# A quarter turn of an 8192 x 8192 matrix: two instead of five TensorE outputs in the last macro tile but one, and GpSimd and TensorE loops of seven turns

## The chip, the cores and the metric

The kernel runs on one core of a Trainium2 chip. The metric is the device time of one execution in microseconds (us). Three runs of the kernel before took 1258.8 to 1259.03 us, with a median of 1258.96 us. A profile is one more execution of the same program, recorded instruction by instruction and DMA packet by DMA packet; its own time is given beside its span.

## The reference

What is computed is a rotation by a quarter turn of a float32 matrix. There is no arithmetic in it, only movement: 256 MiB are read and 256 MiB are written.

```python
x = np.random.randn(8192, 8192).astype(np.float32)   # k = 1
def reference(x, k):
    return np.rot90(x, k)
```

Row r and column c of the input go to row 8191 - c and column r of the output. So the kernel has to transpose and to reverse the order of the columns.

## The kernel before

**Tiling.** The matrix is cut into 16 macro tiles of 1024 rows by 4096 columns (`macros`, numbered kk = 0 to 15). A macro tile is loaded in 8 loads of 128 rows by 4096 columns, 2 MiB each (t = 0 to 7), and stored in 8 outputs (j = 0 to 7), each 512 rows of the result by 1024 columns, also 2 MiB. Loads are numbered m = 8 kk + t and outputs n = 8 kk + j, both from 0 to 127. Output n needs a part of all 8 loads of its macro tile. In the steady state the outputs of one macro tile are made while the next one is loaded, so output n goes with load m = n + 8.

**Memory.** There are two landing buffers for loads and three buffers for outputs, 2 MiB each (`bufs`), and `ring`, which holds one macro tile, less one chunk, as 63 chunks of 128 rows by 512 columns. VectorE takes a landed load out of its landing buffer into the ring, with the columns reversed (`landed` has a step of -1). The chunk that does not fit into the ring (t = 7, j = 7) is reversed in place in its landing buffer, and TensorE transposes it from there into `corner`, a piece of PSUM.

**Two ways to make an output.** `by_pe(kk)` says which of the 8 outputs of a macro tile TensorE makes.

- By TensorE: VectorE copies the chunks into the ring; TensorE transposes 32 blocks of 128 x 128 against an identity matrix into the two halves of PSUM (`ps0`, `ps1`); ScalarE copies each filled part to the output buffer (an eviction); then ScalarE issues the store.
- Moved: VectorE transposes the chunks within squares of 32 x 32 on their way into the ring (`in_quadrants`); then 16 copies, each of a band of 32 partitions, bring the squares to their places in the output buffer: 3 by VectorE, 8 by GpSimd, 5 by ScalarE (`moves`, `pairs`). Outputs with j = 7 have 7 tiles in such a copy instead of 8, and the corner is evicted by ScalarE.

In macro tiles 0 and 15 TensorE makes all outputs, in 1 to 13 outputs 0 and 4, and in 14 outputs 0, 2, 4, 6 and 7.

**Order of the work.** Each engine's order is written out by hand.

- SyncE (`by_sync`) issues the loads. Load m waits until VectorE has taken everything out of the same landing buffer (`taken`).
- VectorE (`by_vector`) goes by loads. For load m it first makes its 3 copies of output n = m - 8, if that is a moved one; then waits for the landing; then waits until GpSimd's copies of output n are done (`s_pool`), or, for an output by TensorE, until its transposes are done (`s_half`); then takes the load out, in pieces, each of which counts up `s_rev`. Only then may a chunk of the ring be overwritten, since the ring holds one macro tile.
- GpSimd (`by_gpsimd`) goes by moved outputs: it waits until the output buffer is free (`room_for`), copies 7 times, waits for ScalarE's copies of the same output (`s_act`), and copies once more.
- TensorE (`by_tensor`) goes by its outputs in the order of `in_turn`. For the first two outputs of macro tile 15, `FIRST` = 120 and 121, parts are interleaved: two parts of output 120 (16 and 12 blocks, from loads 120 to 126), a part of 16 blocks of output 121, the last 4 blocks of output 120 (from load 127), and the rest of output 121.
- ScalarE (`by_scalar`) goes by outputs: it makes its share of copies or its evictions, and issues the store. For a moved output it waits, ahead of the store, for the first piece that VectorE takes out of load n + 8: `e.wait_ge(s_rev, rev[n + T, pieces[n + T][0][0]])`. That one wait stands for VectorE's and GpSimd's copies of output n.

All of ScalarE's work for output 120 stands behind the store of output 119.

**Loops.** The instructions of GpSimd, VectorE and TensorE are first recorded (`Program`) and then played. Macro tiles `first` to `first + 2 * times - 1` become a loop of `times` turns of two macro tiles; the rest is written out straight. In a loop every turn must have the same list of operations, and only the numbers that are waited for go up. GpSimd's loop goes over macro tiles 1 to 12, that of VectorE and that of TensorE over 2 to 13. ScalarE has no loop. `once` leaves out a wait for a number that has been waited for before.

A line of the profile such as L104 is the place in `Op.run` from which all recorded operations are issued, so the profile's groups are told apart by engine, operation and tile.

Of the kernel before, what the change touches and what calls it, by code (L numbers as in the profile page):

```python
# [13 lines left out]
J = W // (G * P)  # L14
# [10 lines left out]
BY_PE = [0, 4]  # L25
# [148 lines left out]
def kernel(tc: tile.TileContext, x: bass.AP, k: bass.AP, out: bass.AP):  # L174
    nc = tc.nc
# [6 lines left out]
    KK = len(macros)  # L182
# [13 lines left out]
    def by_pe(kk):  # L196
        if kk in (0, KK - 1):
            return list(range(J))
        return BY_PE if kk < KK - 2 else [*range(0, J, 2), J - 1]

    def in_quadrants(kk, j):
        return j not in by_pe(kk)

    moved = [in_quadrants(kk, js[0]) for kk, _, js, _ in outs]
# [36 lines left out]
    def moved_until(n):  # L241
        return sum(moved[: n + 1])

    def turned_until(n):
        return sum(len(parts[i]) for i in range(n + 1) if i in parts)
# [16 lines left out]
    s_rev = nc.alloc_semaphore("s_rev")  # L262
# [8 lines left out]
    def load_buf(m):  # L271
        if m < T:
            return m % (LAND + OUTS)
        return LAND + 2 if m == T else (m - T - 1) % LAND
# [10 lines left out]
    def once(e):  # L285
        seen = {}

        def wait(sem, n):
            if seen.get(sem, 0) < n:
                seen[sem] = n  # L290
                e.wait_ge(sem, n)

        return wait

    def room_for(wait, n):
        b = out_buf(n)
        stores = [i for i in range(n) if out_buf(i) == b]
        loads = [i for i in range(n_load) if load_buf(i) == b]
        if stores:
            wait(s_store[b], 16 * len(stores))  # L300
        elif loads:
            taken(wait, loads[-1])

    def tight(n):
        return J <= n < n_out - J and n % J == TIGHT
# [24 lines left out]
    for m in range(n_load):  # L330
        kk, t = divmod(m, T)
# [16 lines left out]
    def at(v, first, dims):  # L348
        return bass.AP(
            tensor=v.tensor, offset=v[:, first : first + 1].offset, ap=[v.ap[0], *dims]  # L350
        )

    def landed(b, js):
        return at(bufs[b][:], (js[0] + 1) * CH - 1, [*strides(js, CH), [-1, CH]])

    def chunk(kk, t, js):
        if (kk, t, js[0]) == (KK - 1, T - 1, J - 1):
            return at(ring[:], 0, [[CH, 1], [1, CH]])
        places = [slot(kk, t, j) for j in js]
        assert max(places) < SLOTS  # L360
        return at(ring[:], places[0] * CH, [*strides(places, CH), [1, CH]])

    def moves(n, share):
        kk, ts, (j,), _ = outs[n]
        rows = len(ts) * P
        places = [slot(kk, t, j) for t in ts if (t, j) != (T - 1, J - 1)]
        ((step, tiles),) = strides(places, CH)
        for a, q in share:
            yield (
                at(  # L370
                    bufs[out_buf(n)][q * Q : q * Q + Q, :],
                    a * Q,
                    [[rows, G], [P, tiles], [1, Q]],
                ),
                at(
                    ring[a * Q : a * Q + Q, :],
                    places[0] * CH + q * Q,
                    [[P, G], [step, tiles], [1, Q]],
                ),
            )  # L380
# [26 lines left out]
    def landings(m):  # L407
        return 16 * sum(1 + (i in BOTH) for i in range(m + 1) if load_buf(i) == load_buf(m))

    def turned_in(n):  # L410
        kk, _, (j,), _ = outs[n]
        return rev[kk * T + T - 1 - (j == J - 1), j]
# [37 lines left out]
    def by_vector(e):  # L450
        wait = once(e)
        for m in range(n_load):
            kk, t = divmod(m, T)
            e.part(kk)
            b = load_buf(m)
            n = m - T
            if n >= 0 and moved[n]:
                room_for(wait, n)
                wait(s_rev, turned_in(n))
                for to, of in moves(n, pairs[:BY_DVE]):  # L460
                    i = e.tensor_copy(out=to, in_=of)
                i.then_inc(s_dve, 1)
            e.wait_ge(s_land[b], landings(m))
            if n >= 0:
                if moved[n]:
                    e.wait_ge(s_pool, moved_until(n))
                    e.wait_ge(s_dve, moved_until(n))
                else:
                    e.wait_ge(s_half, turned_until(n))
            for js in pieces[m]:  # L470
                if (m, js[0]) == (n_load - 1, J - 1):
                    e.wait_ge(s_half, turned_until(KK * J - J))
                if kk < KK - 1 and (t, js[0]) == (T - 1, J - 1):
                    wait(s_rev, rev[m, 0])
                    e.tensor_copy(
                        out=at(bufs[b][:], 0, [[CH, 1], [1, CH]]), in_=landed(b, js)
                    ).then_inc(s_rev, 1)
                    continue
                turn = e.transpose if in_quadrants(kk, js[0]) else e.tensor_copy
                turn(out=chunk(kk, t, js), in_=landed(b, js)).then_inc(s_rev, 1)  # L480

    def in_turn():
        for n in parts:
            if n == FIRST[0]:
                early, late = parts[n], parts[FIRST[1]]
                yield n, early[:2]
                yield FIRST[1], late[:1]
                yield n, early[2:]
                yield FIRST[1], late[1:]
            elif n != FIRST[1]:  # L490
                yield n, parts[n]

    def by_tensor(e):
        e.part(-1)
        wait = once(e)
        e.wait_ge(s_id, 2)
        used = {}
        for n, some in in_turn():
            kk, ts, js, blocks = outs[n]
            e.part(kk)  # L500
            rows = len(ts) * P
            order = [(part, f) for part in some for f in part[2]]
            if js[0] == 0 and kk < KK - 1:
                late = parts[n][-1]
                order.sort(key=lambda o: (o[0] == late, o[1] % rows, o[1]))
            last = dict(order)
            for part, f in order:
                _, h, cols = part
                j, off = blocks[f // rows]
                t = ts[f % rows // P]  # L510
                if kk < KK - 1 and js[0] == 0 and f == parts[n][-1][2][0]:
                    m = kk * T + T - 1
                    wait(s_rev, rev[m, J - 1])
                    wait(s_freed, kk)
                    for g in range(G):
                        i = e.transpose(
                            corner[:, g * P : g * P + P],
                            bufs[load_buf(m)][:, g * P : g * P + P],
                            ident,
                        )  # L520
                    i.then_inc(s_corner, 1)
                if n == KK * J - J and h:
                    wait(s_freed, KK - 1)
                if used.get(h, part) != part:
                    wait(s_ev, evicted[used[h][0]] + 1)
                wait(s_rev, rev[kk * T + t, j])
                if part == parts[n][0] and f == last[part] and n != FIRST[1] and not tight(n):
                    room_for(wait, n)
                to = cols.index(f) * P
                i = e.transpose(  # L530
                    ps[h][:, to : to + P],
                    chunk(kk, t, [j])[:, 0, off : off + P],
                    ident,
                )
                if f == last[part]:
                    i.then_inc(s_half, 1)
                    used[h] = part
# [48 lines left out]

    by_sync(nc.sync)
    for e, by, first, times in (
        (nc.gpsimd, by_gpsimd, 1, 6),
        (nc.vector, by_vector, 2, 6),  # L590
        (nc.tensor, by_tensor, 2, 6),
        (nc.scalar, by_scalar, None, 0),
    ):
        program = Program()
        by(program)
        program.play(nc, e, first, times)
# [39 lines left out]
```

## Time and profile before

| what | value |
|---|---|
| median of three runs | 1258.96 us |
| the profiled execution | 1259.08 us |
| its span (first to last record) | 1257.8 us |
| VectorE (DVE) busy | 793.8 us, 63% |
| GpSimd (POOL) busy | 744.0 us, 59% |
| ScalarE (ACT) busy | 599.6 us, 48% |
| TensorE (PE) busy | 302.9 us, 24% |
| read and written in HBM | 268.44 MB each, 427 GB/s over the span |
| loads and stores, issue to landing | 15.0 and 15.8 us (medians) |
| chain that ended last | DMA 71%, DVE 14%, ACT 4%, POOL 4% |

How to read it: the page divides the span into 40 slices of 31.4 us; digits are busy tenths of a slice, and the row of the clock is the TensorE clock that was granted, in tenths of full speed. The timeline lists instructions of one engine in order of time: start in us, duration, engine and line, operation and tiles, the count of merged instructions, and in brackets the idle time before and what ended it. ACTq and SPq are the sequencers of ScalarE and SyncE, which issue DMAs. A load or store is 128 rows of 16,384 bytes or as much, 8 packets for each of the core's 16 DMA engines; the trace holds each packet's start and duration and the moment at which each engine reports its share as landed.

### The profile page before, as it was taken

To read this page: it belongs to the slowest core of one execution; us is meant where nothing else is said; L and a number is where in the kernel's file an instruction comes from. 1 tells how busy PE (TensorE), PEld (TensorE's weight loads), DVE (VectorE), ACT (ScalarE), POOL (GpSimd) and SP (SyncE) were. 2 spreads that over 40 slices of the span, in tenths; PEclk is the share of its full clock that TensorE was granted. 3 is DMA by queue.
4 is the path that set the end of the run, shared out by engine and by line. 5 is a ranking of instruction groups with operands and counts; after the bars stand their busy time and mean duration, and the time that the engine had idled before them with its cause. 6 is when DMAs were issued, how large, how long until landed. Compare 5 with 4: busy or idle time off the path is not lost.

```text
span 1257.8 us, 6012 instructions
## 1 busy us (share of the span) xinstructions
PE 302.9 (24%) x1556; PEld 264.8 (21%) x1556; DVE 793.8 (63%) x535; ACT 599.6 (48%) x556; POOL 744.0 (59%) x654
## 2 busy tenths in 40 slices
PE   1555013130131301313022130221302213024273
PEld 0454012130121301212012120121202212024273
DVE  2544866668666676666867667676677766764410
ACT  0334364463644636446364453645535455355364
POOL 0001966668666686666956668576685766965500
PEclk9987556555555555555556555565555556555597
DMA  9999999999999999999999999999999999999999
GB/s 400 420 430 429 429 429 429 429 431 430 430 430 429 430 428 430 428 430 430 430 430 429 431 428 431 428 430 428 430 430 429 430 429 431 427 423 428 427 428 381
DMA packets 36946, 537.09 MB, mean 427 GB/s; under 512 B 4160, under 2 KB 4160, under 8 KB 4160
## 3 DMA queue, kind: packets, MB, share of 16 engines
q10 hardware_dynamic: 19184, 278.93, 52.2%
q1 hardware_dynamic: 17744, 257.96, 48.0%
q8 instruction: 7, 0.11, 0.0%
q14 instruction: 11, 0.09, 0.0%
HBM read 268.44 MB, written 268.44 MB: 427 GB/s over the span
## 4 chain that ended last, share of the span: by engine, by line
DMA 71%; DVE 14%; ACT 4%; POOL 4%; issue 3%; PE 2%; ACTq 0%; DVEq 0%; SPq 0%; POOLq 0%
DMA buf<-in_x_dram 57%; DMA out_dram<-buf 14%; DVE ring L104 14%; ACT buf L104 4%; POOL buf L104 4%; PE ps L104 2%; ACTq L104 0%; DVE buf L104 0%; DVEq L101 0%; SPq L391 0%; DVEq L145 0%; POOLq L101 0%; SPq L311 0%; POOLq L151 0%; SPq L419 0%
## 5 line engine op out<-in xcount | busy, mean ns | idle before, releaser
L104 POOL COPY buf<-ring 32x1024 f32<-32x1024 f32 (+1 forms) x648 | 743.3, 1147 | 440.4 <-DMA out_dram<-buf 244.2
L104 ACT COPY buf<-ring 32x1024 f32<-32x1024 f32 (+1 forms) x405 | 414.8, 1024 | 324.2 <-DVE ring L104 292.5
L104 PE MATMUL ps<-head,ring 128*128 128x128 f32 x1496 | 290.7, 372 | 889.4 <-ACT buf L104 535.8
L104 PEld LDWEIGHTS ps<-head,ring 128*128 128x128 f32 x1496 | 255.3, 197 | 921.5 <-ACT buf L104 548.7
L104 DVE COPY ring<-buf 128x1024 f32<-128x1024 f32 (+5 forms) x152 | 157.7, 1044 | 415.6 <-DMA buf<-in_x_dram 320.1
L104 DVE STREAM_TRANSPOSE ring<-buf 128x3072 f32<-128x3072 f32 (+2 forms) x125 | 358.0, 2872 | 0.0
L104 ACT COPY buf<-ps 128x2048 f32<-128x2048 f32 (+4 forms) x149 | 183.3, 1278 | 313.6 <-DMA out_dram<-buf 149.3
L104 DVE COPY buf<-ring 32x1024 f32<-32x1024 f32 (+1 forms) x243 | 289.5, 1192 | 2.2
L104 PE MATMUL ps<-head,buf 128*128 128x128 f32 x60 | 15.2, 401 | 46.3 <-DVE buf L104 46.3
L104 PEld LDWEIGHTS ps<-head,buf 128*128 128x128 f32 x60 | 9.7, 199 | 52.0 <-issue 44.6
L104 DVE COPY buf<-buf 128x512 f32<-128x512 f32 x15 | 5.8, 387 | 0.0
L104 ACT ACT_TABLE_LOAD x1 | 1.3, 1283 | 3.4 <-PEq L419 3.4
L104 POOL MEMSET head<- 128x128 f32 x1 | 0.2, 204 | 2.9 <-POOLq L419 2.9
L104 POOL TENSOR_SCALAR_AFFINE_SELECT head<-head 128x128 f32<-128x128 f32 x1 | 0.3, 293 | 0.2 <-POOL head L104 0.2
L617 POOL MEMSET const-float32-0.0<- 128x1 f32 x1 | 0.1, 98 | 0.2 <-issue 0.2
L104 ACT COPY head<-head 128x1 f32<-128x1 f32 x1 | 0.2, 191 | 0.0
L617 POOL MEMSET const-bfloat16-1.0<- 128x1 bf16 x1 | 0.1, 100 | 0.0
L617 POOL MEMSET const-uint8-127<- 128x1 uint8 x1 | 0.1, 100 | 0.0
L617 POOL MEMSET const-float32-1.0<- 128x1 f32 x1 | 0.1, 98 | 0.0
## 6 DMA issues: line engine op xcount, KB each, us to landing
out_dram<-buf ACTq DMA_DIRECT2D x128, 2048.0 KB, 15.8
buf<-in_x_dram SPq DMA_DIRECT2D x121, 2048.0 KB, 15.0
buf<-in_x_dram ACTq DMA_DIRECT2D x3, 2048.0 KB, 16.9
buf<-in_x_dram SPq DMA_DIRECT2D x4, 1024.0 KB, 16.1
buf<-in_x_dram ACTq DMA_DIRECT2D x4, 1024.0 KB, 16.4
```

The lines of the kernel that those rows point to most:

```text
L104: i = getattr(e, self.name)(*self.args, **kwargs)
L617: nc = _bacc.Bacc("TRN2", target_bir_lowering=False, num_devices=1)
```

## The change

In macro tile 14 TensorE makes outputs 0 and 4, as in 1 to 13; outputs 2, 6 and 7 become moved ones. GpSimd's loop goes over macro tiles 1 to 14 in 7 turns, TensorE's over 1 to 14 instead of 2 to 13; VectorE's is as it was. So that every turn has the same list of operations, TensorE forgets at output 8 which numbers it has waited for. VectorE waits, ahead of its copies of a moved output, for the largest count that any moved output of the macro tile needs, instead of the one that this output needs.

```diff
@@ by_pe @@
         if kk in (0, KK - 1):
             return list(range(J))
-        return BY_PE if kk < KK - 2 else [*range(0, J, 2), J - 1]
+        return BY_PE
@@ by_vector @@
             if n >= 0 and moved[n]:
                 room_for(wait, n)
-                wait(s_rev, turned_in(n))
+                wait(s_rev, max(turned_in(i) for i in range(n - n % J, n - n % J + J) if moved[i]))
                 for to, of in moves(n, pairs[:BY_DVE]):
@@ by_tensor @@
             kk, ts, js, blocks = outs[n]
             e.part(kk)
+            if n == J:
+                wait = once(e)
             rows = len(ts) * P
@@ at the end of tile_rot90_kernel @@
-        (nc.gpsimd, by_gpsimd, 1, 6),
+        (nc.gpsimd, by_gpsimd, 1, 7),
         (nc.vector, by_vector, 2, 6),
-        (nc.tensor, by_tensor, 2, 6),
+        (nc.tensor, by_tensor, 1, 7),
         (nc.scalar, by_scalar, None, 0),
```

## The prediction

> **What bounds the kernel now.** I read the slices of the page first, then the chain of waits, then the end in windows of 10 us, then the timelines of ScalarE, GpSimd, VectorE and TensorE over the last macro tiles, and last the records of transfers and packets. The page's slices:
>
> ```profile
> PEclk9987556555555555555556555565555556555597
> DMA  9999999999999999999999999999999999999999
> GB/s 400 420 430 429 429 429 429 429 431 430 430 430 429 430 428 430 428 430 430 430 430 429 431 428 431 428 430 428 430 430 429 430 429 431 427 423 428 427 428 381
> ```
>
> The DMA engines are busy from end to end, and the chain of waits is 71% DMA. No compute engine exceeds 63%. The packet records say it more sharply. A packet of 16,384 bytes starts 3 ns before the one ahead of it on its engine ends, so the records fall into sixteen chains, one for each DMA engine. Each holds about 2048 packets of 0.611 (load) or 0.616 us (store), with hardly a hole. The engines end between 1253.7 and 1257.3 us, and the landing record follows 0.4 us later, 1257.7. So nothing that happens on compute engines costs time unless it leaves DMA engines without a queued transfer, and little can be gained: the sixteen chains hold about 1255 us each.
>
> The end in windows (us, then busy time and count of PE, PEld, DVE, ACT, POOL, then the granted TensorE clock, the DMA share and GB/s):
>
> ```profile
> 1190.00:1200.00 10.00, 5.04 (x25) 4.61 (x25) 2.47 (x2) 4.89 (x5) 0.00 (x0) 0.52 1.01 428
> 1200.00:1210.00 10.00, 6.65 (x57) 5.88 (x56) 2.41 (x3) 5.98 (x5) 0.00 (x0) 1.00 1.00 428
> 1210.00:1220.00 10.00, 8.23 (x72) 7.45 (x71) 1.59 (x2) 7.85 (x5) 0.00 (x0) 1.00 1.01 426
> 1220.00:1230.00 10.00, 8.96 (x79) 8.24 (x77) 0.00 (x0) 8.59 (x5) 0.00 (x0) 1.00 1.01 425
> ```
>
> GpSimd is done, TensorE runs at the full clock, and DMA has no hole. The place where a hole can open is the hand-over from output 119 (last of macro tile 14) to output 120 (first of 15), after the last load landed at 1209.13. ScalarE's timeline there:
>
> ```profile
> 1196.09 0.55 ACTq L104 DMA_DIRECT2D out_dram<-buf  x1
> ...
> 1203.07 0.55 ACTq L104 DMA_DIRECT2D out_dram<-buf  x1
> 1203.94 3.21 ACT L104 COPY buf<-ps 128x2048 f32<-128x2048 f32 x2 [0.90 <-PE ps L104]
> 1210.39 0.58 ACT L104 COPY buf<-ps 128x512 f32<-128x512 f32 x1 [3.24 <-PE ps L104]
> 1211.01 0.55 ACTq L104 DMA_DIRECT2D out_dram<-buf  x1
> 1211.65 3.63 ACT L104 COPY buf<-ps 128x2048 f32<-128x2048 f32 x2 [0.67 <-ACT buf L104]
> ```
>
> The three issues are stores 118, 119, 120. Two evictions of output 120 are done before the last load lands; only a third of 0.58 us follows it. The DMA engines reach store 120's packets at 1214.4 to 1216.9, so the issue at 1211.01 has 3.4 us to spare (less the start-up below). Later issues come every 4.25 us, and an engine takes 4.91 us for its part of a store, so the reserve then grows.
>
> **The change part by part.** In macro tile 14 outputs 2, 6 and 7 leave TensorE and become moved ones. Removed: 96 transposes and their ScalarE evictions (3.70 us for each of outputs 2 and 6). Added: 24 GpSimd copies, 9 VectorE copies, 15 ScalarE copies, and wider VectorE transposes for loads 112 to 119. A load with two outputs by TensorE costs VectorE a copy and a transpose of 3072 (2872 ns mean); loop turns do this at 429 to 430 GB/s, so loads 112 to 119 cost nothing; load issues keep 5 us or more of queued load.
>
> What counts is that a moved output's store waits, in ScalarE's order, for VectorE's first piece of load n+8, and VectorE starts that piece only after GpSimd's last copy of output n. GpSimd in the last macro tile now:
>
> ```profile
> 1138.11 11.63 POOL L104 COPY buf<-ring 32x1024 f32<-32x1024 f32 x8 [8.21 <-DMA out_dram<-buf]
> 1157.66 21.13 POOL L104 COPY buf<-ring 32x1024 f32<-32x1024 f32 x15 [7.92 <-DMA out_dram<-buf]
> 1186.81 1.03 POOL L104 COPY buf<-ring 32x1024 f32<-32x1024 f32 x1 [8.02 <-ACT buf L104]
> ```
>
> Outputs 113, 115, 117 come singly, with holes of 8 us. One takes 11.63 us here: seven copies of 1.03 or 1.40 and one of 3.00 beside VectorE's 128x4096 copy. Loads land every 9.78. With the change they come as 113-114-115 and 117-118-119.
>
> First row, from 1138.11: ends 1149.7, 1161.4, 1173.1. Loads 122 and 123 landed at 1160.07 and 1169.85, so VectorE is 1.3 and 3.2 us late; stores 114 and 115 go out at 1163.8 and 1175.5 (before: 1156.95, 1172.56). Store 114 moves until 1177.15 and load 124 until 1179.59 on the last engine, so at most half a microsecond of hole on fast engines: priced at nothing, since they end 3 us ahead of the slowest. If that cover were gone it would cost those 0.5 us.
>
> Second row. Output 117 ends at 1187.84 as now (its eighth copy waits for ScalarE). Output 118 follows: +11.7 = 1199.6; load 126 landed 1199.25. Load 126's VectorE copy then meets GpSimd's first copy of output 119 and ends about 1202.9 rather than 1201.57; store 118 issues at 1203.0. Output 119 has copies of seven tiles: 0.93 or 1.23, and about 2.9 beside the 128x4096 copy, 10.8 in all: 1210.5 (ScalarE's own part ends at 1208.9). So GpSimd, not the landing at 1209.13, releases the last load. VectorE's first piece 0.44: ScalarE issues store 119 at 1211.05.
>
> Then all of output 120's evictions lie behind that wait, which they did not before. Issue and start of a copy 0.60: 1211.65. First eviction (2048) 1.82: 1213.5. That frees the half of PSUM that TensorE needs for 16 transposes of output 121, which stand ahead of the last 4 of output 120. Their price has two ends in this trace:
>
> ```profile
> 1058.58 5.45 PE L104 MATMUL ps<-head,ring 128*128 128x128 f32 x28 [0.68 <-ACT buf L104]
> ...
> 1205.86 1.97 PE L104 MATMUL ps<-head,ring 128*128 128x128 f32 x16 [0.65 <-ACT buf L104]
> 1209.73 0.63 PE L104 MATMUL ps<-head,ring 128*128 128x128 f32 x4 [1.90 <-DVE ring L104]
> ```
>
> At the half clock (first line, a hand-over inside the loop) one takes 0.195 us, so 20 take 3.9; at full clock 2.6. Now TensorE works on outputs 118 and 119 ahead of 120; after the change it has nothing between output 116 and 120 and pauses again from about 1210 to 1213.5. In the loop the clock record goes to 1.0 for 3.4 us, then back to 0.5 after such a pause. I take the half clock: 1217.45 (full: 1216.15). Last eviction 0.58: **store 120 issues at 1218.1** (full clock 1216.8).
>
> From issue to first packet: the launch's first load, on empty engines, is issued at 0.91 and its sixteen first packets start at 1.96 to 2.52, that is 1.05 to 1.6; I take 1.3. So store 120's packets start at 1219.4, where the engines ran out of store 119 at 1217.3 to 1217.5 (1211.05 + 1.3 + 4.91, or on the slowest what was queued). From there an engine needs 39.26 us for its eight parts (so it does now), and 41.22 if a page of TensorE's code is fetched through it meanwhile: now two engines in the tail have that, a packet of 0.95 us and a hole of 1.0 after it. TensorE's pages come every 125 transposes or so (the records have them after 100, 229, 372, and behind the loop 471, 588, 729 of the program's transposes), and outputs 120 to 127 hold 256, so one still falls in the tail. Now the slowest engine is another (40.41, from 1216.90, delayed by ScalarE's pages); the one that takes TensorE's page becomes the slowest. 1219.4 + 41.2 + 0.4 for the landing = 1261.0, against 1257.7: **+3.3 us**.
>
> The other edits. Loop turns of TensorE and GpSimd over 1 to 14: some register instructions, on engines that are idle (TensorE 24% busy); no more than tenths of a microsecond each way, hidden behind DMA. VectorE's two waits on its own counter become one, for pieces finished a load earlier; a wait in the chain is 0.02 to 0.05 us. TensorE's forgotten waits at output 8 are for events long past. About two of the 7 TensorE pages go and a GpSimd page; the slowest engine took none of them, so 0, with 2 us as the end if it had.
>
> **The rivals.**
> - *Quick hand-over, no measurable difference.* If GpSimd is done by the landing and TensorE has the full clock: store 119 at 1209.75, store 120 at 1215.5, packets at 1216.8, end 1258.4: +0.7. It decides at an issue of store 120 at 1217.3: below, the loss is under 2.5 us. For it: full clock at 1200 to 1230 now, and each GpSimd row is my sum, not a row of the trace. Against: the clock in the loop's hand-over, and the copies of 3.00. Between the two lies +2.0 (GpSimd late, full clock).
> - *A second gap.* Output 121 needs 16 more cold transposes and its second eviction: issue about 1223.2, packets 1224.5, while store 120 is through at 1224.3. With first packets at 1.06 instead of 0.61 us, as at launch: +4.5.
> - *Code loading.* TensorE's loop body (136 transposes) begins 68 transposes earlier, and might straddle pages so that each turn fetches. The row: over 230 to 1100 us the instruction queue of TensorE moved nothing, in six turns whose body is longer than a page. If two pages were fetched in each of seven turns, 14 times 1.96 us over sixteen engines is one or two for each: another +2 to +4.
>  The Trainium skill ("Runtime: NRT & Kernel Launch", Instruction fetch mechanics) says that a taken branch whose target is outside the two-page window forces a fetch, and prefers unrolling. By that rule this change costs in each turn; the trace's six silent turns speak against it.
> - *Faster.* If a page less falls on the slowest engine: -1 to -2 us at most, and only with the quick hand-over.
>
> That the change does not do what it says is excluded by the order of instructions: the built kernel's loops and copies are as described.
>
> **How the numbers follow.** The profiled execution took 1259.08 us, with a span of 1257.8; the median is 0.12 lower. 1259.08 + 3.3 - 0.12 = 1262.3; I say 1262.2. 0.2% is 2.5 us, about what a measurement here can tell from no change. Chances: forecast 0.45, second gap 0.07, code loading 0.04: slower 0.56. Quick or half-quick hand-over 0.42: same. Faster 0.02. The range runs from the quick hand-over, 1259.6, to just short of the second gap's full price, 1263.6.
>
> **What would show it.** In the changed profile: GpSimd busy to about 1210.5; VectorE waiting there for GpSimd, not for the load; stores 119 and 120 issued near 1211 and 1218; TensorE's clock near half between 1210 and 1217; the DMA share of 1210 to 1220 near 0.6 instead of 1.01; and pure stores from there at the old pace. If the DMA share stays at 1 there, the hand-over was covered and the forecast is wrong. If the instruction queue of TensorE shows tens of packets, it was code loading. A loss before 1200 us would be a step that I priced at nothing.

## The result, and the profile after

The changed kernel takes 1264.31 us (median of 6 runs, 1262.97 to 1265.18) against 1258.88 (6 runs, 1258.55 to 1259.03). The ratio is 1.0042, 95% interval 1.0031 to 1.0053: slower by 5.4 us, where 3.3 were forecast, and outside the stated range. The profiled execution, 1265.18 us with a span of 1263.9, is the longest of the six.

The page's slices of the changed kernel show where the time went. Until about 1137 us (slice 36) they are within 2 GB/s of those of before; then the rate falls.

```profile
DMA  9999999999999999999999999999999999999989
GB/s 398 422 431 431 428 429 428 431 430 428 429 429 431 430 428 429 429 431 431 428 429 430 431 430 429 429 430 430 431 428 429 430 431 430 426 421 415 403 369 393
```

In windows of 10 us (columns as in the prediction), the first two lines from the kernel before, the others from the changed one:

```profile
1160.00:1170.00 10.00, 2.71 (x16) 2.47 (x14) 7.31 (x5) 2.86 (x3) 9.73 (x7) 0.67 1.00 424
1170.00:1180.00 10.00, 0.90 (x4) 0.71 (x4) 2.53 (x1) 2.82 (x2) 8.54 (x7) 0.50 1.01 424
```

```profile
1150.00:1160.00 10.00, 0.00 (x0) 0.00 (x0) 7.16 (x4) 5.21 (x5) 9.71 (x8) 0.50 1.02 421
1160.00:1170.00 10.00, 0.00 (x0) 0.00 (x0) 7.45 (x4) 5.21 (x5) 9.73 (x7) 0.50 0.97 385
1170.00:1180.00 10.00, 0.00 (x0) 0.00 (x0) 3.16 (x1) 1.45 (x1) 9.65 (x9) 0.50 0.97 377
...
1210.00:1220.00 10.00, 7.23 (x40) 6.99 (x38) 2.11 (x3) 5.00 (x4) 3.24 (x4) 0.69 0.77 328
1220.00:1230.00 10.00, 7.94 (x69) 7.14 (x68) 0.41 (x1) 7.87 (x5) 0.00 (x0) 1.00 0.80 337
```

There are two troughs. The second, 1210 to 1230, is the hand-over of the forecast: the DMA share (second number from the end) falls to 0.77 and 0.80. The first, 1160 to 1180, was priced at nothing. The share there hides most of it: it is 0.97, but the rate is 377 to 385 instead of 424 GB/s. The packet records say why. Of 492 load packets begun between 1150 and 1187 us, 86 took 0.70 to 2.0 us instead of 0.61 (before the change 7 of 499); all 86 began within 6 us of the issue of load 123, 124 or 125. That is 2.2 us per engine, in which it counts as busy and moves less. Idle time is another 0.9 us.

GpSimd, ScalarE and VectorE in this stage:

```profile
1137.55 44.54 POOL L104 COPY buf<-ring 32x1024 f32<-32x1024 f32 x31 [8.06 <-DMA out_dram<-buf]
1188.28 1.04 POOL L104 COPY buf<-ring 32x1024 f32<-32x1024 f32 x1 [6.18 <-ACT buf L104]
1191.20 22.16 POOL L104 COPY buf<-ring 32x1024 f32<-32x1024 f32 x16 [1.89 <-DMA out_dram<-buf]
```

```profile
1175.86 0.55 ACTq L104 DMA_DIRECT2D out_dram<-buf  x1
...
1205.88 0.55 ACTq L104 DMA_DIRECT2D out_dram<-buf  x1
...
1213.91 0.55 ACTq L104 DMA_DIRECT2D out_dram<-buf  x1
1214.50 3.21 ACT L104 COPY buf<-ps 128x2048 f32<-128x2048 f32 x2 [2.69 <-DVE ring L104]
1220.42 0.59 ACT L104 COPY buf<-ps 128x512 f32<-128x512 f32 x1 [2.71 <-PE ps L104]
1221.03 0.55 ACTq L104 DMA_DIRECT2D out_dram<-buf  x1
```

```profile
1172.67 3.16 DVE L104 COPY ring<-buf 128x4096 f32<-128x4096 f32 x1 [4.22 <-POOL buf L104]
...
1213.45 2.10 DVE L104 COPY ring<-buf 128x512 f32<-128x512 f32 x2 [3.79 <-POOL buf L104]
```

The four issues are stores 115, 118, 119 and 120. VectorE waits for GpSimd, not for the load, both in the first row (load 123) and at the last load. GpSimd's 24 copies of outputs 113 to 115 and the first 7 of output 117 run without a hole; its second row, outputs 118 and 119, starts at 1191.20, released by a store (115, which landed at 1191.05; before the change it landed at 1186.96), and ends at 1213.36. Store 120 is issued 7.1 us after store 119, at 1221.03, and by then the engines are empty. They were empty once before: of the 4.4 us for which an engine stands idle here, half lies ahead of store 119's first packets and half ahead of store 120's.

### The profile page after: what moved, and what is told of

It reads as the page before. It is cut to its first block, busy times and chain, and to the rows that moved or that the text cites. A ratio compares the mean times of both kernels' runs of the same rounds, so it can differ in the third digit from the quotient of the medians.

```text
span 1263.9 us, 5913 instructions
## 1 busy us (share of the span) xinstructions
PE 288.2 (23%) x1464; PEld 252.8 (20%) x1464; DVE 791.7 (63%) x538; ACT 604.0 (48%) x562; POOL 765.7 (61%) x678
## 4 chain that ended last, share of the span: by engine, by line
DMA 71%; DVE 13%; POOL 5%; issue 4%; ACT 4%; PE 1%; ACTq 0%; DVEq 0%; POOLq 0%; SPq 0%
DMA buf<-in_x_dram 56%; DMA out_dram<-buf 15%; DVE ring L104 13%; POOL buf L104 5%; ACT buf L104 4%; PE ps L104 1%; ACTq L104 0%; DVEq L101 0%; DVE buf L104 0%; POOLq L101 0%; SPq L391 0%; POOLq L151 0%; POOLq L145 0%; SPq L419 0%; ACTq L101 0%
## 5 line engine op out<-in xcount | busy, mean ns | idle before, releaser
L104 POOL COPY buf<-ring 32x1024 f32<-32x1024 f32 (+1 forms) x672 | 765.0, 1138 | 444.2 <-DMA out_dram<-buf 235.6
L104 ACT COPY buf<-ring 32x1024 f32<-32x1024 f32 (+1 forms) x420 | 429.9, 1024 | 353.6 <-DVE ring L104 324.3
L104 PE MATMUL ps<-head,ring 128*128 128x128 f32 x1404 | 275.8, 375 | 909.5 <-ACT buf L104 570.4
L104 PEld LDWEIGHTS ps<-head,ring 128*128 128x128 f32 x1404 | 243.2, 199 | 938.8 <-ACT buf L104 578.0
L104 DVE COPY ring<-buf 128x1024 f32<-128x1024 f32 (+2 forms) x145 | 146.8, 1015 | 426.3 <-DMA buf<-in_x_dram 352.2
L104 DVE STREAM_TRANSPOSE ring<-buf 128x3072 f32<-128x3072 f32 (+2 forms) x126 | 370.2, 2947 | 0.0
L104 ACT COPY buf<-ps 128x2048 f32<-128x2048 f32 (+3 forms) x140 | 172.7, 1279 | 290.1 <-DMA out_dram<-buf 139.0
L104 DVE COPY buf<-ring 32x1024 f32<-32x1024 f32 (+1 forms) x252 | 286.3, 1136 | 2.3
```

Of the source, the lines that this page charges most:

```text
L104: i = getattr(e, self.name)(*self.args, **kwargs)
```

## The experiments

Each ran beside the kernel before; a ratio is to that kernel, with its 95% interval. Two quantities from the packet records of each profile go with the times: packets per DMA engine begun between 1150 and 1187 us (60.4 before the change, so each one less is 0.61 us lost), and idle time per engine between 1205 and 1232 us (none before).

| kernel | median, us | ratio (interval) | packets 1150-1187 | idle 1205-1232, us |
|---|---|---|---|---|
| the change | 1264.31 | 1.0042 (1.0031 to 1.0053) | 55.6 | 4.4 |
| two outputs only | 1263.67 | 1.0036 (1.0022 to 1.0050) | 55.3 | 4.2 |
| loops only | 1258.73 | 0.9999 (0.9990 to 1.0008) | 59.5 | 0.0 |
| outputs 0, 4, 7 | 1260.83 | 1.0015 (1.0006 to 1.0024) | 56.4 | 0.7 |
| outputs 0, 2, 4 | 1261.94 | 1.0025 (1.0016 to 1.0034) | 59.8 | 3.6 |
| other shares | 1264.41 | 1.0040 (1.0026 to 1.0053) | 55.5 | 3.9 |
| plain order | 1263.57 | 1.0038 (1.0024 to 1.0051) | 54.6 | 2.9 |
| other shares, plain order | 1264.19 | 1.0045 (1.0032 to 1.0059) | 56.3 | 4.0 |
| other shares, direct wait | 1259.44 | 1.0003 (0.9994 to 1.0012) | 60.6 | 1.3 |
| two pieces | 1261.62 | 1.0023 (1.0014 to 1.0032) | 57.6 | 2.7 |
| direct wait | 1261.13 | 1.0020 (1.0010 to 1.0029) | 60.1 | 3.0 |
| two pieces, other shares | 1261.05 | 1.0018 (1.0009 to 1.0027) | 60.7 | 3.4 |
| other shares, direct wait, plain order | 1258.89 | 1.0000 (0.9991 to 1.0009) | 60.6 | 1.2 |

**Two outputs only, and loops only.** They part the change in two. The first is the kernel before with `return BY_PE` in `by_pe`. The second is the kernel before with these edits:

```diff
-                wait(s_rev, turned_in(n))      # VectorE
+                wait(s_rev, max(turned_in(i) for i in range(n - n % J, n - n % J + J) if moved[i]))
+            if n == J:                          # TensorE
+                wait = once(e)
-        (nc.tensor, by_tensor, 2, 6),
+        (nc.tensor, by_tensor, 1, 6),
```

> Macro tile 14 as in the change (TensorE makes outputs 0 and 4), all loops and waits as before the change (GpSimd 1 to 12, TensorE 2 to 13, VectorE waits for each output's own count). Theory (GpSimd comes late in two rows of three moved outputs, and the DMA engines run dry after the first row and at the hand-over from output 119 to 120): 1264.3 us, as the change itself, within 1 us. Rival (the loops: code pages, extra waits): 1258.9 us, as before.

> The loops and waits alone: five outputs by TensorE in macro tile 14 as before, but TensorE's loop begins at macro tile 1 (six turns, 1 to 12), it forgets its waits at output 8, and VectorE waits once for the largest count. Theory (GpSimd's rows): 1258.9 us, within 0.3. Rival (the loops): 1261 to 1264 us.

The outputs carry the cost, and the moved loop of TensorE with the other waits none: as the theory had it. The seventh turns of GpSimd and TensorE need the new macro tile 14 and stand in neither run. The change itself has them, and its time (1264.31 against 1263.67 with two outputs only) is within both intervals.

**Outputs 0, 4, 7 and outputs 0, 2, 4.** Each breaks one of GpSimd's two rows of three moved outputs.

```diff
-        return BY_PE if kk < KK - 2 else [*range(0, J, 2), J - 1]
+        return BY_PE if kk < KK - 2 else [0, 4, 7]        # the other: [0, 2, 4]
```

> Loops as before; TensorE makes outputs 0, 4 and 7 of macro tile 14. GpSimd's first row of three stays (113 to 115), the second is 117 and 118 alone, and output 119 needs no GpSimd. Theory that both rows cost: a hole near 1166 to 1181 us as in the change, none at the hand-over, 1260 us within 0.7. Rival that only the hand-over costs and the first row is free: 1258.9 to 1259.2 us.

> Loops as before; TensorE makes outputs 0, 2 and 4 of macro tile 14. The first row is broken (113 and 115 come singly), the second stays (117 to 119). This is the prediction's second row with a punctual start: GpSimd from 1187.9 to about 1210.5, store 120 issued at 1217 to 1218, 1261 to 1262.3 us. Rival that a late first row is the whole cause: 1258.9 to 1259.5 us.

Both rows cost: the first 2.0 us, the second 3.1, together nearly the 5.4 of the change. Outputs 0, 4, 7 came 0.1 us above their range, and the hand-over was not free there, as had been expected: store 120 went at 1216.77 and the engines stood idle for 0.7 us. So the 2.0 us are not the first trough alone. With outputs 0, 2, 4 the second row is the one of the prediction, with a punctual start. GpSimd and ScalarE there:

```profile
1186.27 23.36 POOL L104 COPY buf<-ring 32x1024 f32<-32x1024 f32 x17 [7.96 <-ACT buf L104]
```

```profile
1202.16 0.55 ACTq L104 DMA_DIRECT2D out_dram<-buf  x1
...
1210.17 0.55 ACTq L104 DMA_DIRECT2D out_dram<-buf  x1
...
1216.72 0.55 ACTq L104 DMA_DIRECT2D out_dram<-buf  x1
```

GpSimd ends at 1209.6 (1210.5 forecast), store 119 goes at 1210.17 (1211.05) and store 120 at 1216.72 (1218.1). Store 121 followed only 5.6 us later, at 1222.36, and the engines were idle again ahead of it, for 0.8 us.

**Other shares, plain order, both.** If GpSimd's 11.6 us per output were what delays the rows, 6 copies instead of 8 should end it. And if 20 transposes at half clock ("cold" in what follows) lengthen the hand-over, output 121's 16 should go behind.

```diff
+    def cuts(n):                       # used wherever pairs[...] is cut
+        late = n // J == KK - 2
+        return (BY_DVE + late, BY_DVE + BY_POOL - late)
```

```diff
-            order = [seen, seen + 1, seen + 3] if n == FIRST[0] else [seen - 1, seen + 1]
+            order = [seen + i for i in range(len(spans))]
...
-                yield n, early[:2]
-                yield FIRST[1], late[:1]
-                yield n, early[2:]
-                yield FIRST[1], late[1:]
+                yield n, early
+                yield FIRST[1], late
```

> The change, but for macro tile 14 alone GpSimd makes 6 of the 16 copies of a moved output, VectorE 4 and ScalarE 6 (elsewhere 8, 3, 5); GpSimd's loop ends at 12, so that this can be. An output then costs GpSimd about 9.3 us instead of 11.6, under the 9.8 us between two loads. Theory (late GpSimd rows are the larger part, ScalarE's order and TensorE's half clock at the hand-over the rest): GpSimd done before each landing, no hole near 1166 to 1181, store 120 at 1215.5 to 1217, 1259.8 to 1261 us. Rival that GpSimd's lateness is all of it: 1258.9 us within 0.3. Rival that it is the number of moved outputs, whoever copies: 1263 to 1264 us.

> The change, but TensorE and ScalarE take outputs 120 and 121 one after the other: the 16 transposes of output 121 no longer stand ahead of the last 4 of output 120. GpSimd stays late. Theory (20 cold transposes between two evictions are part of the hand-over's price): store 120 leaves about 2 to 3 us sooner after store 119, and the time falls to 1262.2 us within 1. Rival that the engines would have stood idle there anyway: 1264 us.

> The shares of copies of the run with 6 for GpSimd together with outputs 120 and 121 in plain order. Theory: store 119 at 1209.7, store 120 near 1215.0, 1259.3 us within 0.4. Rival that GpSimd's lateness was all: 1258.9 us, no different from the shares alone.

The first and third expectation failed: the shares changed nothing. So GpSimd's own pace was not, or not alone, what held the row. The rival that only the number of moved outputs counts came closest; the direct wait below, with as many of them, refutes it. The run with other shares shows what did. VectorE, ScalarE and GpSimd in it:

```profile
1160.97 3.15 DVE L104 COPY ring<-buf 128x4096 f32<-128x4096 f32 x1 [3.82 <-POOL buf L104]
...
1172.22 3.15 DVE L104 COPY ring<-buf 128x4096 f32<-128x4096 f32 x1 [2.33 <-POOL buf L104]
```

```profile
1164.15 0.55 ACTq L104 DMA_DIRECT2D out_dram<-buf  x1
1164.74 6.30 ACT L104 COPY buf<-ring 32x1024 f32<-32x1024 f32 x6 [4.95 <-DVE ring L104]
1175.40 0.55 ACTq L104 DMA_DIRECT2D out_dram<-buf  x1
```

```profile
1171.10 8.39 POOL L104 COPY buf<-ring 32x1024 f32<-32x1024 f32 x6 [1.76 <-ACT buf L104]
```

It is a ring of waits. VectorE takes load 122 out (1160.97 to 1164.12); only then may store 114 go (1164.15); only behind it come ScalarE's copies of output 115 (1164.74 to 1171.04); GpSimd, which has been waiting for them (1.76 us idle), makes its last copy (from 1171.10); only then may VectorE take load 123 out (1172.22). One turn is 11.25 us, against 9.8 between loads. In the change, with ScalarE's 5.25, the ring is about 10.5 and GpSimd's eight copies 11.6; taking copies from GpSimd and giving one to ScalarE shortened one and lengthened the other. In the loop the first piece is 2 chunks (0.7 to 1.3 us), so that the same ring adds up to less than 9.8 us; in the last macro tile it is all 8 (2.3 to 3.2).

Plain order did shorten the step from store 119 to 120, from 7.1 to 5.6 us, and the idle time from 4.4 to 2.9, of which 1.6 us now lie ahead of store 121. But the time is just outside what was expected, and within the intervals of the change, so a gain isn't shown.

**Other shares with a direct wait.** This cuts the ring: the store waits for the copies themselves.

```diff
-                e.wait_ge(s_rev, rev[n + T, pieces[n + T][0][0]])
+                if n // J == KK - 2:
+                    e.wait_ge(s_pool, moved_until(n))
+                    e.wait_ge(s_dve, moved_until(n))
+                else:
+                    e.wait_ge(s_rev, rev[n + T, pieces[n + T][0][0]])
```

> The shares of copies of the run with 6 for GpSimd, and ScalarE's store of a moved output of macro tile 14 waits for GpSimd's and VectorE's copies themselves, not for the first piece of load n + 8. So store 119 and the first two evictions of output 120 no longer stand behind the last landing. Theory: store 119 near 1206, store 120 near 1211 as before the change, no hole, 1258.9 us within 0.4. Rival that TensorE's five outputs were needed for another reason: 1260 us or more.

The cost is gone within what can be measured, though the median is 0.1 us above what was expected and a hole of 1.3 us is left at the hand-over, where none was expected (stores 119 and 120 at 1207.44 and 1214.38). ScalarE's timeline:

```profile
1148.16 0.55 ACTq L104 DMA_DIRECT2D out_dram<-buf  x1
...
1159.11 0.55 ACTq L104 DMA_DIRECT2D out_dram<-buf  x1
...
1168.26 0.55 ACTq L104 DMA_DIRECT2D out_dram<-buf  x1
```

Stores 113 to 115 go 1.1 to 2.3 us ahead of the landings that they would have had to wait for (1150.4, 1160.2, 1169.9), and the first trough is gone.

**The ring and GpSimd's pace taken apart.** Two pieces shorten the ring and leave GpSimd's eight copies; a direct wait alone cuts it and leaves them; two pieces with other shares bring both under 9.8 us and keep the wait for the load.

```diff
-            got = [here] if t < T - 1 else [here[:wide], here[wide:-1], here[-1:]]
+            got = [here[:2], here[2:]] if t < T - 1 else [here[:wide], here[wide:-1], here[-1:]]
```

> The change, but VectorE takes loads 120 to 126 out of the landing buffer in two pieces (2 chunks, then 6) instead of one of 8. New theory (a ring of waits: store n waits for VectorE's first piece of load n + 8, ScalarE's copies of output n + 1 come behind that store, GpSimd's last copy waits for them, VectorE's next first piece waits for GpSimd; with a first piece of 8 chunks of 3.1 us, a store issue and a start of 0.6, ScalarE's 5.3 and GpSimd's 1.4 one turn of the ring is 10.5 us, and GpSimd's own eight copies are 11.6, both above the 9.8 between loads): the ring falls to about 8.6, GpSimd's 11.6 stays, 1261 to 1262.5 us. If the ring alone sets it: 1259.5 us. If only GpSimd's copies do: 1263 to 1264 us.

> The change, but ScalarE's store of a moved output of macro tile 14 waits for GpSimd's and VectorE's copies, not for load n + 8; shares 8, 3 and 5 as in the change; GpSimd's loop ends at 12. The ring is cut, GpSimd's 11.6 us stay: it ends output 119 near 1210 instead of 1213. New theory (ring and GpSimd's copies both): 1260.5 to 1261.5 us. If the ring is all: 1259.4 us, as with the shares changed too. If GpSimd's copies are all: 1263 to 1264 us.

> The change with both: loads 120 to 126 in two pieces, and shares of 6 for GpSimd, 4 for VectorE, 6 for ScalarE in macro tile 14. The store still waits for load n + 8. One turn of the ring is then 1.3 + 0.6 + 6.3 + 1.4 = 9.6 us and GpSimd's copies 9.3, both under 9.8. New theory: no hole near 1166 to 1181, store 119 near 1210, store 120 at 1215.5 to 1217, 1259.8 to 1261 us. If the wait for the load as such is the cause, whatever the length of the ring: 1263 to 1264 us.

All three fall to 1261.1 to 1261.6, the first two inside the new theory's ranges, the third a shade above. With both limits under 9.8 us the first trough is gone entirely (60.7 packets), without touching the wait. With the direct wait alone it is gone too (60.1 packets), although GpSimd is as slow as in the change. Its copies, and the windows of the first trough:

```profile
1137.43 46.47 POOL L104 COPY buf<-ring 32x1024 f32<-32x1024 f32 x31 [8.29 <-DMA out_dram<-buf]
```

```profile
1160.00:1170.00 10.00, 0.00 (x0) 0.00 (x0) 7.45 (x4) 5.21 (x5) 9.73 (x7) 0.50 1.01 433
1170.00:1180.00 10.00, 1.11 (x4) 0.71 (x4) 3.16 (x1) 3.52 (x3) 9.65 (x9) 0.50 0.99 423
```

VectorE takes loads 122 and 123 out at 1160.83 and 1172.52, as late as in the change (1160.97 and 1172.67), but stores 114 and 115 go at 1160.78 and 1172.46, 3.4 us sooner than there (1164.16 and 1175.86). So late loads alone do not open the trough; stores that are held back with them are part of it. Late stores alone were not tried. The time of this run fits the new theory, but not for its reason: what is left of the loss is the hand-over, with 3.0 us of idle time.

The hand-over is also what remains with two pieces and other shares. Its stores 119 and 120:

```profile
1209.48 0.55 ACTq L104 DMA_DIRECT2D out_dram<-buf  x1
1216.56 0.55 ACTq L104 DMA_DIRECT2D out_dram<-buf  x1
```

Even with everybody on time, output 120's evictions behind the last landing and TensorE's cold 20 transposes keep store 120 until 1216.6. The engines stand idle for 3.4 us, 2.1 of them ahead of store 120's packets and the rest ahead of store 119's.

**The candidate for the fastest** has other shares, the direct wait and the plain order.

> Shares of 6, 4 and 6 in macro tile 14, its stores waiting for the copies themselves, and outputs 120 and 121 in plain order: the candidate for the fastest. Store 120 is then no longer behind 16 transposes of output 121. Expected: 1258.9 us within 0.4, the same as before the change, since the DMA engines hold 1254 to 1257 us of packets whatever the order; 1257.5 us or less if the order of outputs had cost the kernel before something.

It is no faster than the kernel before, nor slower. No version beats it: the engines are full from 10 to 1205 us in both, but for 0.3 us each.

## Why the prediction was wrong

The direction and the chief mechanism were right; the size was 3.3 us where 5.4 were measured, and one step failed.

- **The step that failed: "priced at nothing" for GpSimd's first row (113 to 115).** Its times were right: stores 114 and 115 were forecast at 1163.8 and 1175.5 and went at 1164.16 and 1175.86. What they do to the DMA engines was not. I compared them with the landings of the kernel before on the slowest engine and allowed "at most half a microsecond of hole on fast engines". In fact store 114 and load 124 are issued together, at 1164.16 (the same VectorE piece releases both), and land together, at 1178.5 and 1178.4. So both queues of an engine run out together, and many of the load packets after that are long: 4.8 packets per engine lost between 1150 and 1187 us, 2.9 us. Outputs 0, 4, 7, which keep this row whole and have 0.7 us of idle time at the hand-over, cost 2.0 us.
- **The same step left out a wait.** Output 118 needs the output buffer of store 115, and the prediction itself moved that store from 1172.56 to 1175.5. Yet it let output 118 follow 117 at 1187.9, "as now". Store 115 landed at 1191.05, 4.1 us later than before, and GpSimd's second row started at 1191.20. It took 22.2 us (22.7 forecast), so it ended 2.9 us late, and that lateness runs through to the end.
- **Second row and hand-over: right as a path, in part by luck as a price.** Measured alone, with outputs 0, 2, 4, 3.1 us against 3.3. But there store 120 went 1.4 us sooner than forecast, and the 0.8 us ahead of store 121 made up for part of it. That is the prediction's second gap, which had a chance of 0.07: it opened with outputs 0, 2, 4 and with two outputs only (0.7 us), not in the profile of the change. In the changed kernel everything is 2.9 us later, for the reason above, but every distance holds: GpSimd's end to store 119 0.55 us (0.55 forecast), store 119 to 120 7.1 (7.05), store 120 to the end of the span 42.8 (42.9). TensorE at half clock, 20 transposes in 3.96 us (3.9 forecast):

```profile
1216.42 3.96 PE L104 MATMUL ps<-head,ring 128*128 128x128 f32 x20 [2.77 <-ACT buf L104]
```

- **Why the row is late: half right.** I had GpSimd's 11.6 us per output. The ring of waits through VectorE's piece of 8 chunks and ScalarE was not seen; in the change it is nearly as long. Shortening one of the two leaves a trough (55.5 packets with other shares, 57.6 with two pieces). It is gone where both are under 9.8 us, and where the store no longer waits for VectorE.
- **Start-up and code page: right.** From store 120's issue to the first packets on fifteen engines 1.21 to 1.36 us (1.3). Two engines end at 1263.3 and 1263.4, the others by 1262.2, twelve of them by 1261.6. Two pages of TensorE's code moved in the tail, at 1222.2 and 1242.5, so the two late engines fit one page each; the forecast was one page, at 1.96.
- **Loops at nothing: right.** 1258.73 with TensorE's loop and the waits alone. TensorE's instruction queue moved 5 pages instead of 7, two of them in the tail, and none from 230 to 1100 us. The page's queues:

```profile
q8 instruction: 5, 0.08, 0.0%
q14 instruction: 10, 0.08, 0.0%
```

 The Trainium skill's rule on taken branches ("Runtime: NRT & Kernel Launch", Instruction fetch mechanics) makes a jump pay only where its target is outside the two-page window. So it does not follow from the rule that each turn costs, as the prediction had it. No page of TensorE's code was fetched between 230 and 1100 us, so no run here shows such a charge.
- **"Loads 112 to 119 cost nothing": right.** The rates until 1130 us are those of before.

Two slips in the rivals do not touch the forecast. The second gap at +4.5 comes to 1263.5, just inside the range's end of 1263.6 and not beyond it. And fourteen code pages over sixteen engines are fewer than one for each, not one or two.

One sum comes close for all versions that lost time. Add the time lost in 1150 to 1187 us (0.61 us per missing packet) and the idle time of 1205 to 1232 us, and set it against the same profiled execution's own time, less the 1258.9 of before: 7.3 against 6.3 us for the change, 3.1 against 2.0 for outputs 0, 4, 7, 4.0 against 2.8 for outputs 0, 2, 4, 4.4 against 3.0 for two pieces, 3.4 against 1.9 for two pieces with other shares, 1.3 against -0.3 for other shares with the direct wait. The measured loss is 1.0 to 1.7 us less each time. For the change most of it is accounted for: the engines ended on average 2.5 us ahead of the slowest one before, and 1.6 after. For the others that is an argument; no run was made to test it alone.

Still open: how much of the changed kernel's spread (1263.0 to 1265.2, against 0.5 us before) comes from where a code page falls. That wasn't tried.

## What to carry to other kernels

Where DMA bounds a kernel, price an edit by the queues of the slowest and of the fastest engine in that stage, not by engine shares: an issue that comes later costs nothing until a queue runs out, and if one event releases a load and a store, both can run out at once. Follow a late store to the next output that needs its buffer. When several engines share the making of one tile, add up the turn of each ring of waits and compare it with the time between transfers; speeding up one member did nothing here, since the ring went on through another. A signal borrowed from a neighbour ("the next load's first piece is out") is free only as long as that piece is short.

## What the runs showed of the hardware

Behind the late issues of loads 123 to 125, 86 load packets took 0.70 to 2.0 us instead of 0.61, so a share of 0.97 went with a rate about 10% lower (377 to 385 GB/s against 424). The store packets behind the two holes of the hand-over took their usual 0.61 to 0.64 us from the first one on. Why only load packets were slow isn't shown. A page of TensorE's code (16 KB) in the tail cost the one DMA engine that fetched it 1.96 us in the kernel before, a packet of 0.95 and a hole of 1.0. In the changed kernel, where the engines started the tail nearly together, the two late engines ended 1.8 to 1.9 us behind the twelve that ended together. GpSimd's copies of 1.03 us took 3.00 beside VectorE's copy of 128 x 4096, 1.40 beside its copies of 32 partitions.
